# Float32r head sums for the removal keys, and mixer steps traced later among the big products, in a hybrid decoder layer

## The chip, the cores and the metric

The kernel runs on one core of one Trainium2 chip. The metric is the device time of one execution in microseconds, as the median of several runs. PE is the matmul engine, DVE the vector engine, ACT the scalar engine, POOL the GpSimd engine; SP is the engine whose queue starts the loads of the weights.

## The reference

One layer for 256 tokens of width 2048, in float32, with `p` the product of the normalised input with `w_in`:

```
x = x + 0.5 * swiglu(rms_norm(x, ffn1_norm), ...)           # inner width 5632
q, k, v, p_rwkv, gates = split(rms_norm(x, mix_norm) @ w_in)
y_attn = sliding_window_attention(q, k, v, sinks)           # 16 heads of 64, window 128
y_rwkv = rwkv7_time_mix(p_rwkv, ...)                        # 16 heads of 64
x = x + (gate_attn * (y_attn @ w_proj_attn) + gate_rwkv * (y_rwkv @ w_proj_rwkv)) @ w_out
x = x + cross_attention(rms_norm(x, cross_norm), mem)       # 256 rows of memory, 4 heads of 128
x = x + 0.5 * swiglu(rms_norm(x, ffn2_norm), ...)
return rms_norm(x, final_norm)
```

Within `rwkv7_time_mix` each of the 1024 columns of `k` is scaled, and then each head of 64 is divided by its length; this is where the sums of the removal keys come from:

```
kk = k * k_k
kk = kk / max(sqrt(sum(kk * kk over the head's 64 columns)), 1e-12)
```

The recurrence over the tokens has `-kk` and `kk * a` as the two vectors by which the state is corrected at each step (`a` and `b` in `S = S * w + (S a) b + v k`).

## The kernel before, in words

**Products.** Every large product is made of float32r matmuls. A value is split into `hi`, its float32r rounding, and `lo`, the rest, also float32r; `times` (L414 to L419) makes three matmuls of 512 columns out of it: `xh` with `hi` (L417), `xh` with `lo` (L418), `xl` with `hi` (L419). The weights come through SP's queue into `raw` tiles (`load`, L324 on), at most four ahead of use, and are split by an ACT copy (L344) and a DVE subtraction (L345), two items ahead of use. The feed-forward parts have their own variant with combined weights (L352, L353); the change does not touch it.

`product` (L393 on) goes through its weight items, each of two chunks of 128 rows. For each item it makes 6 matmuls for the tokens 0 to 127 and 6 for 128 to 255. Such six matmuls are called a **step** here. With `skew=True` the last three items are kept back, and then worked off for the first 128 tokens and afterwards for the others, without a tick.

**Ticks.** After each step `product` calls `bg.tick()`. `bg` holds generators in groups ("feat", "attn", "ew", "chain", "norm", "mem" and so on); a tick advances one to two of each group to its next `yield`. All mixer work that is not a big product is traced in this way, spread among the steps. `idle(n)` is `n` yields. So the yields set how many steps lie between two pieces of work, and the order of tracing gives each engine its in-order queue; a scheduler may move instructions a little against it. PE's queue above all is one line: a matmul that waits holds up the big matmuls behind it.

**The mixer's stages, in order,** run under the products with `w_in`, `w_proj_attn`, `w_proj_rwkv` and `w_out`:

- `shifted` (L910): transposes (in `feat`, L605) and token shift of the rwkv columns. The name "small" is the last 288 columns, needed by the decay.
- `removal_keys` (L1003 to L1072), for two heads' halves `h` in turn, on "ew": `kk`, its squares, the head sums with a constant of ones (`bdones`, L1022), root, maximum and reciprocal, the vectors `at` and `bt`, then in a loop over two blocks of 128 tokens the products of `kk` and `at` (L1059), masked on DVE (L1065) and stored by POOL's queue to `ld` in DRAM.
- `substitute` (L1075 to L1096), behind them on "ew": it loads 32x32 blocks from `ld` into `dl` (L1080, four DMAs of SP's queue), inverts them by forward substitution on DVE (a multiply L1087 and a reduction L1092 for each of 31 rows, a step or two apart) and stores them.
- The products of the attention's gate and of `ya`, the attention's output, with `w_proj_attn` (L1103 to L1113): for each of four column blocks a sigmoid and a DVE multiply (L1112).
- `values` (L1133) with two head sums per half by `head_sums` (L797 to L804, matmul L802) with `bdones_r`, the float32r copy of `bdones`.
- `pairs` (L1201 on), on "chain", two heads' columns at a time: masked products (L1190 the matmul, L1196 the mask on DVE), then the chain of small products which carries the state through both blocks.
- `finish` (L1322 on), on "norm": the group norm of `y` (L1341 root, L1343 reciprocal), the gate product L1349, L1353 to L1360, and the split into `yr` (L610, L611). `yr` is what the products with `w_proj_rwkv` read.
- The products with `w_out` into the `x2` blocks (L1414 to L1426): a DVE sum (L1421), then the next norm's transposes of this block, spawned on "feat".

`halves_of` (L793 to L796) splits a tile into float32r halves: a copy on ACT (L794) and a subtraction on DVE (L795). L1059 and L1190 use 64 rows of PE each, the upper or the lower; two that follow each other on different halves can run beside each other.

Of the kernel before, what the change touches and what calls it, by code (L numbers as in the profile page):

```python
# [8 lines left out]
F32R = mybir.dt.float32r  # L9
# [123 lines left out]
def decoder_layer(ctx: ExitStack, tc: tile.TileContext, a: dict, out: bass.AP):  # L133
# [34 lines left out]
    def idle(n):  # L168
        for _ in range(n):
            yield  # L170


    ones = cpool.tile([P, P], F32, name="ones")
# [17 lines left out]
    def mixer_constants(sp):  # L191
# [30 lines left out]
        for v in (bdones, bdmean):  # L222
            r = sp.tile([P, P], F32R, name="ones_r" + str(len(ones_r)))
            act.copy(r[:], v[:])
            ones_r.append(r)
        return abias, mask3, mask_l, bdones, ones_r, keep

# [544 lines left out]
    with tc.tile_pool(name="mx", bufs=1, reuse_waits="tile") as sp:  # L772
        aligned(sp)
        abias, mask3, mask_l, bdones, (bdones_r, bdmean), keep = mixer_constants(sp)

# [133 lines left out]

        def shifted(tok, cols, mus, outs, name):  # L910
            for q in range(0, len(cols), 2):
                n = len(cols[q : q + 2])
                b = feat(tok, cols[q : q + 2])
                p = sp.tile([P, 2, T + 1], F32, tag="p", name="p", bufs=2)
                pool.memset(p[:, :, 0:1], 0.0)
                act.copy(p[:, :n, 1:], b[:, :n])
                yield
                d = sp.tile([P, 2, T], F32, tag="d", name="d", bufs=2)
                pool.tensor_tensor(d[:, :n], p[:, :n, :T], p[:, :n, 1:], ALU.subtract)
                yield  # L920
                for i in range(n):
                    m = mu[:, mus[q + i] : mus[q + i] + 1]
                    dve.scalar_tensor_tensor(
                        outs[q + i], d[:, i, :], m, p[:, i, 1:], ALU.mult, ALU.add
                    )
            bg.seen.add(name)
# [81 lines left out]
        def removal_keys(h):  # L1008
# [8 lines left out]
            act.activation(sq[:], kk[:], AF.Square)  # L1017
            yield
            for i in (0, 2):
                b = tr()  # L1020
                sq2 = sq[:, i : i + 2, :].rearrange("p c t -> p (c t)")
                pe.matmul(b[:], bdones[:], sq2, start=True, stop=True)  # L1022
                act.activation(sq2, b[:], AF.Sqrt)
                yield
                dve.tensor_scalar(sq2, sq2, 1e-12, None, ALU.max)
                for k in range(2):
                    dve.reciprocal(sq[:, i + k, :], sq[:, i + k, :])
                    yield from idle(2)
# [23 lines left out]
            for c in range(2):  # L1052
# [17 lines left out]
                pool.dma_start(ld[:, o : o + 8, :], lt[:])  # L1070
                yield
            yield  # L1072


        def substitute():  # L1075
            yield from idle(4)
            dl = t4("dl", (P, 32, 32))
# [27 lines left out]
        for n in range(4):  # L1105
            pg = product(n2.x, W["w_in"])
            g = t4("ga", (P, 2, 512))
            for t in range(2):
                act.activation(g[:, t, :], pg[t][:], AF.Sigmoid, scale=n2.r[t])
            pa = product(ya, W["w_proj_attn"])  # L1110
            for t in range(2):
# [22 lines left out]
        def values(h):  # L1134
# [13 lines left out]
            for i in (0, 2):  # L1148
                b = head_sums(
                    bdones_r, [v[:, i : i + 2, :].rearrange("p c t -> p (c t)") for v in kp[h]]  # L1150
                )
                v2 = vv[:, i : i + 2, :]
                dve.tensor_tensor(v2, b[:].rearrange("p (c t) -> p c t", c=2), v2, ALU.mult)
                yield
# [48 lines left out]
        def pairs(h, q):  # L1203
# [11 lines left out]
            for c in range(2):  # L1215
                cs_ = slice(c * P, (c + 1) * P)
                if c == 0:
                    mk = masked(h, js, ((0, 0), (1, 0)))
                    yield
                    later = masked(h, js, ((2, 0), (2, 1)))  # L1220
                    yield
                vp = [vtok[h][:, c, j * P : (j + 1) * P] for j in js]
# [57 lines left out]
                if c == 0:  # L1280
                    mk_next = masked(h, js, ((0, 1), (1, 1)))
                    yield
                b = tr()
# [131 lines left out]
        for n in range(4):  # L1415
# [4 lines left out]
            for t in range(2):  # L1420
                dve.tensor_tensor(s[:, t, :], po[t][:], s[:, t, :], ALU.add)  # L1421
            bg.spawn("feat", n3.block(n, s))
            if n == 0:
# [156 lines left out]
```

## Time and profile before

| what | value |
| --- | --- |
| median of 3 runs | 2251.75 us (2251.66 to 2252.43) |
| the profiled execution | 2252.57 us |
| its span, from the first to the last instruction | 2250.8 us |
| mean granted PE clock | 0.999 |
| busy share: PE, DVE, ACT, POOL | 99%, 79%, 54%, 6% |
| chain that ended last: PE, DVE, DMA | 94%, 3%, 1% |

A row of the timeline has the start in microseconds, the duration, the engine, the line and operation, output and inputs with their shapes, the count of records and, in brackets, how long the engine was idle before it and what released it. The durations of matmuls are modelled and overlap; the distance between two starts is what counts. A matmul of plain float32 leaves two records. The stage table has the stretch, its length, and then for each engine the busy time and the count of records, in the order PE, PEld (weight load), DVE, ACT, POOL, then granted clock, DMA share and GB/s. The chain of waits is the work that ended last, followed back, with start and length.

### The profile page before, as it was taken

Reading aid. Unit: us, or ns where it says so; the run is one execution under the profiler, and the core shown is the slowest. Engines: PE = TensorE matmul, PEld = TensorE weight load, DVE = VectorE, ACT = ScalarE, POOL = GpSimd, SP = SyncE. Lnnn points to the kernel's source line nnn. Section 1 sums busy time; section 2 is a strip of 40 time slices with the busy share of each in tenths; the row PEclk is TensorE's granted clock in tenths of the full one; section 3 lists DMA queues with packets and bytes.
Section 4 is the critical chain, followed back from the end, with each engine's and each line's share of the span. In section 5 each row is a group of like instructions: output and inputs, shape, how many; then the busy total and the mean of one; then the engine's idle time right before and its main releaser. Section 6 shows DMA issues by size and latency. Waiting matters only on the chain.

```text
span 2250.8 us, 28046 instructions
## 1 busy us (share of the span) xinstructions
PE 2235.2 (99%) x10617; PEld 1840.3 (82%) x10617; DVE 1782.0 (79%) x2279; ACT 1226.5 (54%) x1601; POOL 132.6 (6%) x192
## 2 busy tenths in 40 slices
PE   9999999999999999999999999999999999999998
PEld 7888888888888877788888888888888888888886
DVE  7898988998989476887534566557998988998987
ACT  6555555555556467444444446556555555554554
POOL 1000000000001000301220040001000000000002
PEclk9999999999999999999999999999999999999999
DMA  7555555556556544676523476548565565555564
GB/s 263 187 201 201 197 203 202 193 190 216 192 188 205 163 142 150 201 223 212 166 77 109 163 261 227 186 159 284 185 213 187 195 210 194 190 209 200 189 207 147
DMA packets 219143, 432.49 MB, mean 192 GB/s; under 512 B 14107, under 2 KB 16384, under 8 KB 219008
## 3 DMA queue, kind: packets, MB, share of 16 engines
q1 hardware_dynamic: 210432, 404.78, 53.3%
q0 software_dynamic: 8112, 25.12, 3.5%
q8 instruction: 83, 1.36, 0.2%
q10 hardware_dynamic: 464, 0.79, 0.1%
q14 instruction: 52, 0.43, 0.1%
HBM read 417.56 MB, written 13.11 MB: 191 GB/s over the span
## 4 chain that ended last, share of the span: by engine, by line
PE 94%; DVE 3%; DMA 1%; issue 1%; POOL 1%; ACT 0%; SPq 0%; POOLq 0%; DVEq 0%; ACTq 0%
PE acc L417 19%; PE acc L418 19%; PE acc L419 19%; PE mm L419 8%; PE mm L418 8%; PE mm L417 8%; PE tr L605 2%; PE tr L418 2%; PE tr L419 2%; PE tr L417 2%; PE mm L1254 1%; DVE lo L345 1%; PE tr L1190 1%; DMA raw<-in_w_out_dram 0%; PE mm L844 0%
## 5 line engine op out<-in xcount | busy, mean ns | idle before, releaser
L345 DVE TENSOR_TENSOR lo<-raw,hi 128x1024 fp32r<-128x1024 f32 (+1 forms) x770 | 894.5, 1163 | 336.6 <-ACT hi L344 334.4
L344 ACT CAST hi<-raw 128x1024 fp32r<-128x1024 f32 (+1 forms) x770 | 759.3, 997 | 734.7 <-PE acc L419 519.6
L417 PE MATMUL acc<-hi,xhi 128*128 128x512 f32 (+1 forms) x1196 | 474.3, 397 | 2.4 <-ACT xhi L632 1.9
L418 PE MATMUL acc<-lo,xhi 128*128 128x512 f32 (+1 forms) x1196 | 464.8, 389 | 0.0
L419 PE MATMUL acc<-hi,xlo 128*128 128x512 f32 (+1 forms) x1196 | 464.1, 388 | 0.0
L417 PEld LDWEIGHTS acc<-hi,xhi 128*128 128x128 f32 x1196 | 225.0, 188 | 51.4 <-issue 4.0
L419 PEld LDWEIGHTS acc<-hi,xlo 128*128 128x128 f32 x1196 | 224.5, 188 | 46.9 <-DVE xlo L633 1.0
L418 PEld LDWEIGHTS acc<-lo,xhi 128*128 128x128 f32 x1196 | 224.9, 188 | 45.3 <-issue 1.7
L352 ACT CAST thi<-raw 128x1024 fp32r<-128x1024 f32 x172 | 178.9, 1050 | 60.4 <-DVE raw L373 46.5
L353 DVE TENSOR_TENSOR tlo<-raw,thi 128x1024 fp32r<-128x1024 f32 x172 | 208.3, 1220 | 0.7 <-ACT thi L352 0.4
L417 PE MATMUL mm<-hi,xhi 128*128 128x512 f32 x380 | 149.3, 393 | 0.0
L419 PE MATMUL mm<-hi,xlo 128*128 128x512 f32 x380 | 148.2, 390 | 0.0
L418 PE MATMUL mm<-lo,xhi 128*128 128x512 f32 x380 | 148.2, 390 | 0.0
L418 PE MATMUL acc<-lo,hhi 128*128 128x512 f32 x372 | 145.6, 391 | 0.8 <-DVE lo L345 0.8
L419 PE MATMUL acc<-hi,hlo 128*128 128x512 f32 x372 | 145.6, 391 | 0.0
L417 PE MATMUL acc<-hi,hhi 128*128 128x512 f32 x372 | 144.9, 390 | 0.0
L419 PEld LDWEIGHTS mm<-hi,xlo 128*128 128x128 f32 x380 | 71.3, 188 | 14.8
L418 PEld LDWEIGHTS mm<-lo,xhi 128*128 128x128 f32 x380 | 71.4, 188 | 14.5
L417 PEld LDWEIGHTS mm<-hi,xhi 128*128 128x128 f32 x380 | 71.4, 188 | 14.5
L418 PEld LDWEIGHTS acc<-lo,hhi 128*128 128x128 f32 x372 | 69.9, 188 | 15.5 <-DVE lo L345 1.2
L417 PEld LDWEIGHTS acc<-hi,hhi 128*128 128x128 f32 x372 | 69.9, 188 | 14.3
L419 PEld LDWEIGHTS acc<-hi,hlo 128*128 128x128 f32 x372 | 69.9, 188 | 14.0
(392 smaller groups left out, 3511.9 us busy)
## 6 DMA issues: line engine op xcount, KB each, us to landing
raw<-in_ffn_w_up_dram SPq DMA_DIRECT2D x88, 1024.0 KB, 5.4
raw<-in_ffn_w_down_dram SPq DMA_DIRECT2D x88, 1024.0 KB, 5.1
raw<-in_ffn_w_gate_dram SPq DMA_DIRECT2D x84, 1024.0 KB, 5.1
raw<-in_w_in_dram SPq DMA_DIRECT2D x136, 512.0 KB, 3.5
raw<-in_w_out_dram SPq DMA_DIRECT2D x32, 512.0 KB, 4.5
raw<-in_w_proj_attn_dram SPq DMA_DIRECT2D x16, 512.0 KB, 3.9
raw<-in_w_proj_rwkv_dram SPq DMA_DIRECT2D x16, 512.0 KB, 5.7
raw<-in_w_cross_kv_dram SPq DMA_DIRECT2D x16, 512.0 KB, 3.6
```

Source lines behind the costliest of these rows:

```text
L344: at["hi"] = act.copy(hi[:, s], raw[:, s])
L345: at["lo"] = dve.tensor_tensor(lo[:, s], raw[:, s], f32(hi[:, s]), ALU.subtract)
L352: act.copy(hi[:], v[:])
L353: dve.tensor_tensor(lo[:], v[:], f32(hi[:]), ALU.subtract)
L417: pe.matmul(o, xh, hi, start=first, stop=False, **how)
L418: pe.matmul(o, xh, lo, start=False, stop=False, **how)
L419: pe.matmul(o, xl, hi, start=False, stop=last, **how)
L605: pe.transpose(b[:, o : o + P], tok[:, t, col : col + P], ident[:])
L1190: pe.matmul(b[e][:, o : o + P], x1[r, j, cs_], x2[r, j, cs_], start=True, stop=True)
L1254: pe.matmul(vb[:, (o + k) * P : (o + k + 1) * P][:, r], lhs(k, e), rhs[:, k, r], start=first and k + e == 0, stop=True, **ek,)
```

## The change

1. `mixer_constants` no longer returns the plain float32 `bdones` next to its float32r copy; the copy takes the name `bdones`. `values` uses it as before.
2. `removal_keys` splits the squares into float32r halves (`sh`, `sl`, one ACT copy and one DVE subtraction of 128x1024 for each half `h`), waits two ticks in place of one, and makes each of the four sums by `head_sums`, two float32r matmuls, in place of one matmul of plain float32.
3. In the loop over the two blocks `removal_keys` waits two ticks in place of one behind each block.
4. `shifted` begins two ticks later for "small".
5. `substitute` waits ten ticks in place of four before its loads.
6. The fourth product of `ya` with `w_proj_attn` is skewed, so six of its eight steps have no tick.
7. `pairs` waits two ticks in place of one behind the masks `later` and `mk_next`.
8. The norm of each `x2` block is spawned with two ticks of waiting ahead (`later_by`).

In the order of the instructions the counts change by 4 matmuls on PE, 3 instructions on ACT and 2 on DVE.

```diff
+    def later_by(n, steps):
+        yield from idle(n)
+        yield from steps
...
-        return abias, mask3, mask_l, bdones, ones_r, keep
+        return abias, mask3, mask_l, ones_r, keep
...
-        abias, mask3, mask_l, bdones, (bdones_r, bdmean), keep = mixer_constants(sp)
+        abias, mask3, mask_l, (bdones, bdmean), keep = mixer_constants(sp)
...
         def shifted(tok, cols, mus, outs, name):
+            if name == "small":
+                yield from idle(2)
...
             act.activation(sq[:], kk[:], AF.Square)
-            yield
+            sp_ = halves_of(sq[:], t4("sh", dt=F32R)[:], t4("sl", dt=F32R)[:])
+            yield from idle(2)
             for i in (0, 2):
-                b = tr()
                 sq2 = sq[:, i : i + 2, :].rearrange("p c t -> p (c t)")
-                pe.matmul(b[:], bdones[:], sq2, start=True, stop=True)
+                b = head_sums(
+                    bdones, [v[:, i : i + 2, :].rearrange("p c t -> p (c t)") for v in sp_]
+                )
                 act.activation(sq2, b[:], AF.Sqrt)
...
                 pool.dma_start(ld[:, o : o + 8, :], lt[:])
-                yield
+                yield from idle(2)
             yield
...
         def substitute():
-            yield from idle(4)
+            yield from idle(10)
...
-            pa = product(ya, W["w_proj_attn"])
+            pa = product(ya, W["w_proj_attn"], skew=n == 3)
...
                     later = masked(h, js, ((2, 0), (2, 1)))
-                    yield
+                    yield from idle(2)
...
                     mk_next = masked(h, js, ((0, 1), (1, 1)))
-                    yield
+                    yield from idle(2)
...
-            bg.spawn("feat", n3.block(n, s))
+            bg.spawn("feat", later_by(2, n3.block(n, s)))
```

More of the change, by code (lines that the diff above doesn't have):

```diff
@@ L1149, in values @@
                 b = head_sums(
-                    bdones_r, [v[:, i : i + 2, :].rearrange("p c t -> p (c t)") for v in kp[h]]
+                    bdones, [v[:, i : i + 2, :].rearrange("p c t -> p (c t)") for v in kp[h]]
                 )
```

## The prediction

> **What bounds the kernel now.** I read the page first (its engines, clock and chain), then PE's timeline for the gaps between big matmuls, then DVE's and ACT's around each gap.
>
> ```profile
> span 2250.8 us, 28046 instructions
> PE 2235.2 (99%) x10617; PEld 1840.3 (82%) x10617; DVE 1782.0 (79%) x2279; ACT 1226.5 (54%) x1601; POOL 132.6 (6%) x192
> ...
> PEclk9999999999999999999999999999999999999999
> ...
> PE 94%; DVE 3%; DMA 1%; issue 1%; POOL 1%; ACT 0%; SPq 0%; POOLq 0%; DVEq 0%; ACTq 0%
> ...
> L345 DVE TENSOR_TENSOR lo<-raw,hi 128x1024 fp32r<-128x1024 f32 (+1 forms) x770 | 894.5, 1163 | 336.6 <-ACT hi L344 334.4
> L344 ACT CAST hi<-raw 128x1024 fp32r<-128x1024 f32 (+1 forms) x770 | 759.3, 997 | 734.7 <-PE acc L419 519.6
> ```
>
> PE is busy for 99% of the span and the chain that ended last is PE's for 94%. So time comes only from small PE work made cheaper, or from gaps of PE closed, and time goes wherever PE waits anew. The unit is the spacing of big matmuls:
>
> ```profile
> 1293.36 0.39 PE L417 MATMUL acc<-hi,yrhi 128*128 128x512 f32 x1
> ...
> 1301.52 0.39 PE L417 MATMUL acc<-hi,yrhi 128*128 128x512 f32 x1
> ```
>
> These are the first matmul of the product of `yr` and the one 36 later, which first reads the last two of its eight chunks: 8.16 us / 36 = 0.227 us each, and six of them, one step between two ticks, are 1.36 us. The change leaves all 8958 of these big matmuls as they are. A gap is below the distance of two starts less 0.23.
>
> **The change part by part.** The instruction order of the two kernels, compared engine by engine, gives the places.
>
> *Four sums (L1022).* The chain of waits shows one in the old form, and one of L802 in the form that takes its place, on the same tile shape:
>
> ```profile
> 887.85 0.86 PE tr L1022 x2
> ```
>
> ```profile
> 1143.42 0.46 PE tr L802 x2
> ```
>
> 0.40 each, **gain 1.6**. The price is two casts and two subtractions more for the two heads, 2 x (1.0 on ACT + 1.16 on DVE) by the means of L344 and L345, which have the same shape. The stage covers it:
>
> ```profile
> 880.00:955.00 75.00, 74.70 (x362) 59.35 (x361) 64.48 (x70) 40.96 (x48) 17.96 (x13) 1.00 0.61 193
> ```
>
> DVE has 64.5 of 75 us taken, so 2.3 more fit; without that cover a late `lo` would cost up to 2.3. I cost it at nothing.
>
> *Transposes of the small columns (two steps later).*
>
> ```profile
> 815.01 0.40 PE L419 MATMUL acc<-hi,xlo 128*128 128x512 f32 x1
> 816.16 0.33 PE L605 MATMUL tr<-ident,tok 128*128 128x128 f32 x1 [0.75 <-ACT tok L788]
> ...
> 821.21 0.40 PE L419 MATMUL acc<-hi,xlo 128*128 128x512 f32 x1
> ...
> 821.88 0.44 PE L605 MATMUL tr<-ident,tok 128*128 128x128 f32 x2 [0.27 <-DVE yalo L899]
> ```
>
> 1.15 - 0.23 = 0.92 and 0.67 - 0.23 = 0.44. They move by 1 and by 0.5 step (1.36 and 0.68 us), more than the gaps: **gain 1.36**.
>
> *Pair products of the removal keys (L1059), two steps apart instead of one.*
>
> ```profile
> 910.44 1.16 PE L1059 MATMUL mm<-kk,at 64*128 64x128 f32 x16
> ...
> 912.66 0.48 PE L1059 MATMUL mm<-kk,at 64*128 64x128 f32 x2
> 913.43 1.16 PE L1059 MATMUL mm<-kk,at 64*128 64x128 f32 x14 [0.29 <-DVE lt L1065]
> ```
>
> ```profile
> 947.83 1.65 PE L1059 MATMUL mm<-kk,at 64*128 64x128 f32 x16
> ```
>
> The first 16 take 1.16. The second 16 take 1.93 from 912.66 to 914.59, stopped by the masked copy that frees their bank, and the second head's 1.65: 0.77 + 0.49, **gain 1.26**. But in the new order one of the four groups is split by row half, and one pair of another is torn apart, so that there upper and lower 64 rows no longer run side by side. Before there are 16 side-by-side pairs and no single, after it 11 pairs and 10 singles.
>
> ```profile
> 1183.98 1.08 PE tr L1190 x8
> ...
> 1235.90 1.09 PE tr L1190 x16
> ```
>
> Here 8 records (4 matmuls, alone) cost what 16 (4 pairs) cost, 0.27 a matmul or a pair. So each broken pair costs 0.27: 5 x 0.27, **loss 1.35**. The masks of `pairs` (L1190) go the other way, 29 pairs to 33: 4 x 0.27, **gain 1.08**.
>
> *Masks (`idle(2)` for `yield` in `pairs`).*
>
> ```profile
> 1110.68 0.40 PE L419 MATMUL acc<-hi,xlo 128*128 128x512 f32 x1
> ...
> 1111.39 1.75 PE L1190 MATMUL tr<-rt,kk 64*128 64x128 f32 x16 [0.31 <-DVE mk L1196]
> ...
> 1113.07 0.51 PE L417 MATMUL acc<-hi,xhi 128*128 128x512 f32 x1
> ```
>
> 2.39 from matmul to matmul, against 0.23 + 1.09 without a wait, is 1.07. A step more is 1.36, but the DVE copy it waits for can be late behind a weight's `lo` (1.16) as well. Bounds 0 and 1.07; I take half, **gain 0.5**.
>
> *The fourth product of `ya`, skewed.*
>
> ```profile
> 1018.68 0.39 PE L419 MATMUL acc<-hi,xlo 128*128 128x512 f32 x1
> 1019.49 0.50 PE L417 MATMUL acc<-hi,xhi 128*128 128x512 f32 x1 [0.43 <-DVE ga L1112]
> ```
>
> ```profile
> 1007.33 0.81 DVE L1087 TENSOR_TENSOR tmp<-xt,dl 128x625 f32<-128x625 f32 x1
> 1008.17 0.81 DVE L1092 TENSOR_REDUCE xt<-tmp 128x25 f32<-128x625 f32 x1
> ...
> 1018.75 1.28 DVE L1112 TENSOR_TENSOR ga<-acc,ga 128x512 f32<-128x512 f32 x2
> ```
>
> The next product waits for the banks that L1112 reads: 0.81 - 0.23, **gain 0.58**, as the first half now ends 18 matmuls (4.08 us) ahead. The skewed passes have no ticks, so all mixer work behind them comes 6 steps later, beside the six of `substitute` and the three more of each `removal_keys`: 18 in all. And DVE has its 0.64 multiply, two L1087 and one L1092 of about 0.83 and then a `lo` of 1.16 in a row: 4.3 us from 0.17 after the first pass (a matmul's record less its spacing), with gaps 4.6, while PE wants that `lo` at 4.08 + 0.23 = 4.31. **Loss 0.3** (0 to 1.2, one `lo`).
>
> *Blocks loaded six later.* The four loads of `dl` pass six weight loads in SP's queue. PE waits for neither in this stretch and DVE's substitution starts later as a whole: nothing either way. Its cover is the chain behind it, which is the next term.
>
> *The end of the chain.* 18 steps and some later, the last `finish` comes to the product of `yr`. Before, its last product L1349 starts at 1265.76; its result is needed at 1301.52, 28 us of slack.
>
> ```profile
> 1265.76 1.89 PE L1349 MATMUL tr<-xs,g 128*128 128x256 f32 x8
> ```
>
> ```profile
> 1263.96 3.35 DVE L1343 RECIPROCAL sq<-sq 128x512 f32<-128x512 f32 x1 [0.23 <-ACT sq L1341]
> ...
> 1269.82 0.87 DVE L1360 SCALAR_TENSOR_TENSOR yq<-yq,rv,tr 128x256 f32<-128x256 f32 x2
> ...
> 1273.00 0.69 DVE L611 TENSOR_TENSOR yrlo<-yq,yrhi 128x512 fp32r<-128x512 f32 x1 [1.18 <-ACT yrhi L610]
> ```
>
> ```profile
> 1270.47 1.28 ACT L1382 ACT_TABLE_LOAD   x1 [0.34 <-PE acc L419]
> 1271.77 0.69 ACT L1382 ACTIVATE gr<-acc,rs 128x512 f32<-128x512 f32 x1
> 1272.36 0.61 ACT L610 CAST yrhi<-yq 128x512 fp32r<-128x512 f32 x1
> ```
>
> In the new order L1349 stands 22 steps later (29.9 us), at step 829 of a need at 832; the scheduler puts 7 matmuls of the next product ahead of that need. From L1349's start PE has 1.5 (itself) + 3 x 1.36 + 7 x 0.227 = 7.2 us of work. The chain took 4.93 from there to the end of L1360. It gets one `lo` more (1.16), and its square root now stands on ACT behind the gates' ACTIVATEs and a table load, from 0 to 3.8 us (2 x 1.28 + 2 x 0.6); I take 1.8. With the cast of 0.61 and 0.1 to release it: 4.93 + 1.16 + 1.8 + 0.7 = 8.6, so PE waits 1.4. Behind it on PE stands the whole rest of the product. **Loss 1.4**, bounds 0 and 1.4 + 2.0 + 0.8 (a later `yrlo`) = 4.2.
>
> The Trainium skill, page "ScalarE: Activation LUTs", section "What ACT_TABLE_LOAD costs", puts a drain of about 1380 ns beside each load of 1283 ns. The trace has the 1.28 us load, but the ACTIVATE at 1271.77 stands directly behind it, so the row speaks for no drain; with two drains the tail would, by an estimate from that page, be 2.8 us later and the sum -1.8.
>
> *`x2` blocks two steps later.*
>
> ```profile
> 1363.60 0.39 PE L419 MATMUL acc<-hi,mtlo 128*128 128x512 f32 x1
> ...
> 1365.60 0.48 PE L417 MATMUL acc<-hi,mthi 128*128 128x512 f32 x1
> ...
> 1366.85 0.39 PE L419 MATMUL acc<-hi,mtlo 128*128 128x512 f32 x1
> ...
> 1367.43 0.48 PE L417 MATMUL acc<-hi,mthi 128*128 128x512 f32 x1
> ```
>
> Four transposes take 2.00 at the first block, when they wait for the sum on DVE, and 0.58 where they don't: **gain 1.42**. Those of the memory's and the last blocks then share a step: **loss 0.2** (0 to 0.5).
>
> **Sum.** Gains 1.60 + 1.36 + 1.26 + 1.08 + 0.5 + 0.58 + 1.42 = 7.80; losses 1.35 + 0.3 + 1.4 + 0.2 = 3.25; net -4.55. The profiled execution took 2252.57 us, its span and 1.77 around it, so it becomes 2248.0. The median of the runs is 0.82 below it: 2247.2.
>
> **The rivals.**
> 1. *The tail is hidden.* If ACT's order lets the square root through at once, the tail and the skew's `lo` cost nothing, and the masks' wait goes wholly: -4.55 - 1.4 - 0.3 - 0.57 = -6.8, 2244.9; without the other small losses 2243.7. For it: 28 us of slack before, and an estimate that is short by only 1.4.
> 2. *The waits only move.* The closed gaps are 1.36 + 1.26 + 0.58 + 0.5 + 1.42 = 5.1. Each wait is for an engine that also makes `hi` and `lo`; if half of them come back at the next step or as a late `lo`, it is 2249.8, if all, 2252.3. Against it: each move is longer than its gap.
> 3. *The tail decides, and the kernel is slower.* The last `finish` is in one line with PE once it is late: each us of it is one of the span. If its square root stands behind the whole ACT block (3.8), its reciprocal behind one more `lo` and the cast behind one `hi` and one more `lo` (3.3), PE waits 1.4 + 2.0 + 1.16 + 3.3 = 7.9 and the kernel ends at 2253.7. It is slower from a wait of 6.0 on. For it: the chain has no slack left; against it: two of its bounds must fall together. The Trainium skill, "TensorE: Matmul & The Clock Gate", section "What's actually happening", lets an idle window of about 3.4 us halve PE's clock, which would lengthen such a wait; here the granted clock is 9 in all 40 slices and no gap above reaches 2 us, so no row shows it.
> 4. *The sums do not get faster* in the new form, though the row of L802 has the same shape: 2248.8.
>
> **How the numbers follow.** The forecast has 0.36 (2246 to 2248.5), the hidden tail 0.25, the waits that move 0.23, the slow tail 0.13, the sums 0.03. A measurement of this kernel tells about 0.2%, 4.5 us, from no change; that border is 2247.25, in the middle of the forecast. Faster by more: 0.25 and somewhat over half of 0.36, 0.46; slower by more than 4.5 (past 2256.25): a third of the slow tail and a little for what I have not seen, 0.08; the rest, 0.46, is the same. The range goes from the hidden tail without small losses, 2243.7, to the upper bounds of tail, `lo` and masks together, -4.55 + 2.8 + 0.9 + 0.5 + 0.3 = 0, 2251.7.
>
> **What would show it.** The sums at L802 with 0.46 each at four more places. No bracket at the small columns' transposes, at the first `x2` transposes and at the first matmul after `ya`'s fourth product. L1059 in groups with 0.27 for each matmul that stands alone. A gap of 1 to 2 us ahead of the first matmul on the last chunk of `yr`, released by `yrhi`; none speaks for rival 1, one over 6 for rival 3. New brackets at L417 or L418 released by `hi` or `lo` between steps 573 and 900 speak for rival 2. The forecast is wrong if the big matmuls' spacing changes anywhere, or if a `raw` transfer releases PE.

## The result and the profile after

The changed kernel takes 2257.67 us (median of 7 runs, 2255.8 to 2260.36), the kernel before 2251.75 us (7 runs, 2251.32 to 2252.88). The ratio is 1.0026, 95% interval 1.0016 to 1.0036: slower by 5.9 us, where 4.6 us less were forecast. The profiled execution took 2256.07 us, 3.50 more than that of before.

The page of the changed kernel: span, engines, the shares of the chain that ended last.

```profile
span 2254.4 us, 28045 instructions
...
PE 2235.0 (99%) x10617; PEld 1839.1 (82%) x10617; DVE 1788.1 (79%) x2281; ACT 1230.6 (55%) x1604; POOL 131.5 (6%) x192
...
PE 94%; DVE 3%; issue 1%; ACT 1%; DMA 1%; SPq 0%; POOLq 0%; POOL 0%; DVEq 0%; ACTq 0%
```

PE's busy time is 0.2 us less and the span 3.6 us more, so in this execution the loss is in waits of PE. (Lines of the changed kernel stand 4 to 8 further down: L421 to L423 are the three matmuls, L348 and L349 `hi` and `lo`, L806 the head sums, L1067 the pair products, L1095 and L1100 the substitution's rows.) The view of PE's waits from 890 to 1420 us lists them, with the total, the times and the longest (before, the same view has four groups, together 2.0 us):

```profile
PE acc L422 <- DVE lo L349: 2.5, 2, 2.1
PE mm L1067 <- DVE lt L1073: 1.4, 1, 1.4
PE acc L421 <- ACT hi L348: 0.8, 1, 0.8
PE acc L421 <- DVE x L1429: 0.8, 1, 0.8
PE tr L1198 <- DVE mk L1204: 0.7, 2, 0.4
PE acc L421 <- ACT yrhi L614: 0.6, 1, 0.6
PE acc L421 <- DVE ga L1120: 0.5, 1, 0.5
```

The 8958 big matmuls are the same in both, so the start of the n-th can be compared. This table gives changed minus before at quiet places, and from that what each stretch cost (a step is six big matmuls):

| stretch of steps | what lies in it | forecast, us | measured, us |
| --- | --- | --- | --- |
| 560 to 605 | small columns' transposes | -1.36 | -0.53 |
| 605 to 645 | four sums, first half's pair products | -1.60 and about 0 | -1.82 |
| 645 to 660 | a wait for `hi`, second half's pair products | about 0 | +3.30 |
| 660 to 690 | first rows of the substitution | 0 | +2.46 |
| 690 to 705 | skewed product: `lo`, then `ga` | +0.3 and -0.58 | +0.64 and -0.59 |
| 705 to 845 | masks, pairs, last `finish` | -1.58 and +1.4 | +0.58 |
| 845 to the end | `x2` | -1.22 | -0.59 |

In the stretch with the last `finish`, the steps 830 to 836 cost 1.3 around the wait for `yrhi` (0.6 in its bracket, the rest in the gaps beside it); that leaves -0.8 for masks and pairs.

**The first loss (step 654).** PE, then DVE, then POOL of the changed kernel around 953:

```profile
957.07 1.16 PE L1067 MATMUL mm<-kk,at 64*128 64x128 f32 x8 [1.39 <-DVE lt L1073]
```

```profile
952.70 0.68 DVE L1120 TENSOR_TENSOR ga<-acc,ga 128x512 f32<-128x512 f32 x1
953.30 3.11 DVE L349 TENSOR_TENSOR lo<-raw,hi 128x1024 fp32r<-128x1024 f32 x1
956.34 1.27 DVE L1073 TENSOR_TENSOR lt<-mm,mask_l 128x512 f32<-128x512 f32 x2
```

```profile
952.96 2.36 POOL L1057 TENSOR_TENSOR kt<-kt,aa 128x1024 f32<-128x1024 f32 x1 [30.92 <-DVE aa L1053]
...
956.06 2.57 POOL L1058 TENSOR_TENSOR aa<-kt,cs 128x1024 f32<-128x1024 f32 x1
```

PE waits for the masked copy that frees its bank. That copy stands on DVE behind a `lo` that takes 3.11 us in place of 1.2. It ends at 956.41, which is 1.09 after POOL's product ends (955.32), so it looks as if the `lo` only began its work then. Both have two inputs in SBUF. The Trainium skill, page "SBUF — State Buffer", section "Who interferes with whom", says that such a pair shares a read port, that the one that starts first has it for its whole instruction, and that the other blocks; the trace agrees to 0.1 us. Before, `lo` came directly behind the scaling of `aa` and began first, and POOL's product was the longer one; DVE, then POOL of the kernel before:

```profile
945.16 1.38 DVE L1045 TENSOR_SCALAR aa<-aa,rv,ok_a 128x256 f32<-128x256 f32 x4
946.46 1.22 DVE L345 TENSOR_TENSOR lo<-raw,hi 128x1024 fp32r<-128x1024 f32 x1
```

```profile
946.72 3.18 POOL L1049 TENSOR_TENSOR kt<-kt,aa 128x1024 f32<-128x1024 f32 x1 [26.31 <-PE mm L1059]
```

Now `ga`'s multiply stands between, and POOL begins first.

**What else lies in the 3.30 (step 647).** PE and ACT of the changed kernel around 940, then ACT of the kernel before:

```profile
942.82 0.50 PE L421 MATMUL acc<-hi,xhi 128*128 128x512 f32 x1 [0.82 <-ACT hi L348]
```

```profile
936.05 1.28 ACT L1031 ACT_TABLE_LOAD   x1
937.35 0.60 ACT L1031 ACTIVATE sq<-tr 128x512 f32<-128x512 f32 x1
937.96 1.28 ACT L1117 ACT_TABLE_LOAD   x1
939.26 0.69 ACT L1117 ACTIVATE ga<-acc,rs 128x512 f32<-128x512 f32 x1
939.84 2.93 ACT L348 CAST hi<-raw 128x1024 fp32r<-128x1024 f32 x3
```

```profile
938.07 1.26 ACT L1109 ACTIVATE ga<-acc,rs 128x512 f32<-128x512 f32 x2
```

PE waits 0.82 for the last of three `hi`, and the stretch loses 1.1 there with the gap behind it. Before, the two sigmoids of `ga` stand together on ACT. Now a root of the head sums stands between them, with a table load of 1.28 on either side, and the three `hi` wait behind all of it. So of the 3.30, 1.1 is this wait and 1.39 the wait of the first loss. The other 0.8 is in the second group of pair products: what were 16 records side by side are now 8 and 8 alone, 1.1 us more, and one more turn between big and small matmuls, less the 0.5 that PE waited within this group before.

**The second loss (step 677).** PE, DVE and ACT around 989:

```profile
988.64 0.61 PE L421 MATMUL acc<-hi,xhi 128*128 128x512 f32 x2
991.40 0.50 PE L422 MATMUL acc<-lo,xhi 128*128 128x512 f32 x1 [2.14 <-DVE lo L349]
```

```profile
984.76 0.69 DVE L1120 TENSOR_TENSOR ga<-acc,ga 128x512 f32<-128x512 f32 x1 [1.77 <-PE acc L423]
986.12 0.69 DVE L1120 TENSOR_TENSOR ga<-acc,ga 128x512 f32<-128x512 f32 x1 [0.67 <-PE acc L423]
986.73 0.15 DVE L1095 TENSOR_TENSOR tmp<-xt,dl 128x1 f32<-128x1 f32 x1
...
989.69 0.23 DVE L1095 TENSOR_TENSOR tmp<-xt,dl 128x64 f32<-128x64 f32 x1
990.12 1.22 DVE L349 TENSOR_TENSOR lo<-raw,hi 128x1024 fp32r<-128x1024 f32 x1 [0.20 <-ACT hi L348]
```

```profile
983.40 1.05 ACT L348 CAST hi<-raw 128x1024 fp32r<-128x1024 f32 x1 [1.67 <-PE acc L423]
```

The `hi` of this item was ready at 984.45. Its `lo` starts at 990.12 (the bracket names a later `hi`). In DVE's order there stand ahead of it the two multiplies of `ga`, which wait for the end of a product, and then 15 instructions of the first eight rows of the substitution, 3.2 us in one piece. In the kernel before only one of these instructions comes ahead of the next `lo`, then six:

```profile
971.13 0.15 DVE L1087 TENSOR_TENSOR tmp<-xt,dl 128x1 f32<-128x1 f32 x1
972.59 1.23 DVE L345 TENSOR_TENSOR lo<-raw,hi 128x1024 fp32r<-128x1024 f32 x1 [1.30 <-ACT hi L344]
```

### The profile page after: what moved, and what is told of

Its sections match the earlier page's. It is cut to its first block, busy times and chain, and to the rows that moved or that the text cites. A ratio compares the mean times of both kernels' runs of the same rounds, so it can differ in the third digit from the quotient of the medians.

```text
span 2254.4 us, 28045 instructions
## 1 busy us (share of the span) xinstructions
PE 2235.0 (99%) x10617; PEld 1839.1 (82%) x10617; DVE 1788.1 (79%) x2281; ACT 1230.6 (55%) x1604; POOL 131.5 (6%) x192
## 3 DMA queue, kind: packets, MB, share of 16 engines
q8 instruction: 83, 1.36, 0.2%
## 4 chain that ended last, share of the span: by engine, by line
PE 94%; DVE 3%; issue 1%; ACT 1%; DMA 1%; SPq 0%; POOLq 0%; POOL 0%; DVEq 0%; ACTq 0%
PE acc L421 19%; PE acc L423 19%; PE acc L422 19%; PE mm L422 8%; PE mm L423 8%; PE mm L421 8%; PE tr L609 2%; PE tr L422 2%; PE tr L421 2%; PE tr L423 2%; PE mm L1262 1%; DVE lo L349 1%; PE tr L1198 1%; PE mm L848 0%; DMA raw<-in_w_out_dram 0%
## 5 line engine op out<-in xcount | busy, mean ns | idle before, releaser
L349 DVE TENSOR_TENSOR lo<-raw,hi 128x1024 fp32r<-128x1024 f32 (+1 forms) x770 | 897.0, 1167 | 340.3 <-ACT hi L348 338.4
L348 ACT CAST hi<-raw 128x1024 fp32r<-128x1024 f32 (+1 forms) x770 | 759.3, 997 | 737.2 <-PE acc L423 534.7
L421 PE MATMUL acc<-hi,xhi 128*128 128x512 f32 (+1 forms) x1196 | 472.9, 396 | 2.9 <-ACT xhi L636 1.6
L423 PE MATMUL acc<-hi,xlo 128*128 128x512 f32 (+1 forms) x1196 | 464.4, 389 | 0.0
L421 PEld LDWEIGHTS acc<-hi,xhi 128*128 128x128 f32 x1196 | 224.9, 188 | 51.5 <-issue 3.0
L423 PEld LDWEIGHTS acc<-hi,xlo 128*128 128x128 f32 x1196 | 224.5, 188 | 47.1 <-DVE xlo L637 1.0
L421 PE MATMUL mm<-hi,xhi 128*128 128x512 f32 x380 | 149.3, 393 | 0.0
L423 PE MATMUL mm<-hi,xlo 128*128 128x512 f32 x380 | 148.2, 390 | 0.0
L423 PE MATMUL acc<-hi,hlo 128*128 128x512 f32 x372 | 145.5, 391 | 0.0
L421 PE MATMUL acc<-hi,hhi 128*128 128x512 f32 x372 | 144.9, 390 | 0.0
L423 PEld LDWEIGHTS mm<-hi,xlo 128*128 128x128 f32 x380 | 71.3, 188 | 14.9
L421 PEld LDWEIGHTS mm<-hi,xhi 128*128 128x128 f32 x380 | 71.4, 188 | 14.5
L421 PEld LDWEIGHTS acc<-hi,hhi 128*128 128x128 f32 x372 | 69.9, 188 | 14.3
L423 PEld LDWEIGHTS acc<-hi,hlo 128*128 128x128 f32 x372 | 69.9, 188 | 13.9
```

The lines of the kernel that those rows point to most:

```text
L348: at["hi"] = act.copy(hi[:, s], raw[:, s])
L349: at["lo"] = dve.tensor_tensor(lo[:, s], raw[:, s], f32(hi[:, s]), ALU.subtract)
L421: pe.matmul(o, xh, hi, start=first, stop=False, **how)
L423: pe.matmul(o, xl, hi, start=False, stop=last, **how)
```

## The experiments

Each edit is against the changed kernel, or against the run named. The runs are called e1 to e12 below: e1 and e2 move the loads and the substitution, e3 POOL's products, e4 takes one tick back, e5 has the sums alone, e6 the small columns and `x2`; e7, e8, e10, e11 and e12 start from e4 (substitution, skew, masks, `x2`, substitution), and e9 from e5. Every median is of 11 runs; the kernel before ran beside them, with medians of 2252.1, 2251.72 and 2251.91 in the three groups.

### The loads of dl six steps earlier, the rows traced where they were

```diff
         def substitute():
-            yield from idle(10)
+            yield from idle(4)
...
-            yield from idle(14)
+            yield from idle(20)
             tmp = t4("tmp", (P, 32, 32))
```

> The changed kernel with the loads of dl issued after 4 ticks as before the change, and 20 ticks in place of 14 behind them, so that the substitution itself is traced where the change puts it. In the order of DVE its first eight rows then follow six lo's and no longer stand behind the two multiplies of ga. Theory A (a lo stands in DVE's queue behind ga's multiply, which waits for the end of a product, and behind eight rows of the substitution): the 2.14 us wait of PE for lo at 988.9 goes, the span is 2.2 to 2.5 us shorter than the changed kernel's, some 2253.7 by its profiled run. Theory B (the loads of dl themselves collide with the weights on their way): they still pass the queue at a busy place, and a wait of 1 us or more for a raw or a lo stays near the loads. The last finish stays where the change has it, so its waits of about 1.5 us stay. If the lower granted clock of the other runs of the changed kernel (0.996 to 0.998, up to 4 us longer) comes from the long wait at 988.9, the runs lie within 1 us of each other here; if it comes from the waits of the last finish, they still spread over 3 to 4 us.

2254.03 us (2253.34 to 2256.61). The wait at step 677 is gone: the stretch 660 to 690 costs 0.0 in place of 2.46. Though the rows are traced at the old place, they are scheduled earlier with their loads: they run from 976.28, behind six `lo` and ahead of both multiplies of `ga`, in place of 986.73. In the changed kernel `dl` had landed by 979.67, 7 us ahead of its rows, so the loads did not hold them up there. So the order on DVE was the cause. The expectation on the spread fell: the runs still lie 3.3 us apart, so the long wait at 989 alone does not make it. The trace shows another place, in the stage table (granted clock: third figure from the end of the row):

```profile
958.00:958.50 0.50, 0.50 (x3) 0.41 (x2) 0.50 (x1) 0.00 (x0) 0.50 (x1) 0.56 0.90 156
...
961.00:961.50 0.50, 0.50 (x3) 0.40 (x2) 0.50 (x1) 0.00 (x0) 0.36 (x1) 0.53 0.77 164
```

Here the clock is near half of full from 958.1 to 961.5, behind the first wait, the 1.39 us at the pair products, and the stretch 645 to 660 costs 4.9 in place of 3.3.

### All of the substitution six steps earlier

```diff
-            yield from idle(10)
+            yield from idle(4)
```

> The changed kernel with substitute's idle(10) back at idle(4): loads, substitution and all behind them six steps earlier. Theory A: the wait at 988.9 goes (2.4 us) and the last finish is done six steps ahead of need, so its waits (1.5 us) go too: about 3.9 us less than the changed kernel, some 2252.2 by its profiled run, and no run with a lower clock. Rival (the end of the chain has hardly a part in it): the same as the run with the loads alone earlier, within 0.5 us.

2253.59 us (2252.19 to 2255.65), span 3.7 us below the changed kernel's; the 2.46 at the rows are gone, and the stretch 705 to 845 is at -0.25 in place of +0.58. In it the steps 830 to 836 cost 0.0 in place of 1.3, but masks and pairs gain 0.25 in place of 0.8. Between this run and the one before, only 0.8 us of that stretch tells, and 0.4 by the medians: the tail is a small matter. The spread of 3.5 us is there without any wait for `yrhi`, so the last `finish` alone is not what makes it, and the expectation that no run would have a lower clock fell.

### POOL's products behind the masked copies

```diff
-            for i in range(4):
-                c = 4 * h + i
-                dve.tensor_scalar(
-                    aa[h][:, i, :], aa[h][:, i, :], k_a[:, c : c + 1], ok_a[:, c : c + 1],
-                    ALU.mult, ALU.add,
-                )
-            pool.tensor_tensor(kt[h][:], kt[h][:], aa[h][:], ALU.mult)
-            pool.tensor_tensor(aa[h][:], kt[h][:], ei[:], ALU.mult)
             for c in range(2):
...
                 yield from idle(2)
+            for i in range(4):
+                c = 4 * h + i
+                dve.tensor_scalar(
+                    aa[h][:, i, :], aa[h][:, i, :], k_a[:, c : c + 1], ok_a[:, c : c + 1],
+                    ALU.mult, ALU.add,
+                )
+            pool.tensor_tensor(kt[h][:], kt[h][:], aa[h][:], ALU.mult)
+            pool.tensor_tensor(aa[h][:], kt[h][:], ei[:], ALU.mult)
             yield
```

> The changed kernel with the scaling of aa (L1053) and POOL's two products (L1057, L1058) traced behind the loop of the pair products, so that they start after the masked copies. Theory A (POOL's product, begun at 952.96, holds up the lo that DVE begins at 953.30 until it has ended, 3.11 us in place of 1.2, so the masked copy behind it and PE wait): that lo takes 1.2, the wait of 1.39 us at the pair products goes, 1.4 us less, 2256.3; a lo that meets POOL later takes 2 to 3 us, at a place where no PE waits. Rival (the order on DVE, with two multiplies of ga ahead, makes the masked copy late): the wait stays at 1 us or more. The wait at 988.9 and the spread of the runs stay as they are.

2253.81 us (2253.26 to 2256.1). DVE and POOL of this run:

```profile
952.15 1.21 DVE L349 TENSOR_TENSOR lo<-raw,hi 128x1024 fp32r<-128x1024 f32 x1
...
960.71 2.08 DVE L349 TENSOR_TENSOR lo<-raw,hi 128x1024 fp32r<-128x1024 f32 x1 [1.27 <-ACT hi L348]
```

```profile
958.38 3.32 POOL L1077 TENSOR_TENSOR kt<-kt,aa 128x1024 f32<-128x1024 f32 x1
```

The first `lo` takes 1.21 again, though both multiplies of `ga` still stand ahead of it, so the rival falls. The stretch 645 to 660 costs 1.1 in place of 3.3, and that is the wait for `hi` at step 647 alone. The later `lo` meets POOL and ends at 962.79, again 1.09 after POOL's product (961.70), and PE doesn't wait for it. So POOL's product beside the `lo` was the cause of the 1.39 us. (The edit also takes most of the scaling of `aa` from ahead of the masked copy; but the hold of 3.11 - 1.2 = 1.9 is by itself longer than the wait.) In this trace the long wait of step 677 is followed by a slow stretch of PE:

```profile
989.38 0.50 PE L422 MATMUL acc<-lo,xhi 128*128 128x512 f32 x1 [2.15 <-DVE lo L349]
...
990.20 0.57 PE L422 MATMUL acc<-lo,xhi 128*128 128x512 f32 x1
...
993.55 0.45 PE L422 MATMUL acc<-lo,xhi 128*128 128x512 f32 x1
```

```profile
990.00:990.50 0.50, 0.50 (x3) 0.42 (x2) 0.50 (x1) 0.00 (x0) 0.00 (x0) 0.75 0.37 49
...
993.50:994.00 0.50, 0.50 (x3) 0.41 (x2) 0.00 (x0) 0.50 (x1) 0.00 (x0) 0.83 0.87 324
```

From about 990.2 to 993.6 the clock is 0.50. The eight matmuls from 990.20 to 993.55 take 3.35 us in place of 8 x 0.227 = 1.82: 1.5 us lost. That is also why the profile of this run is only 0.8 us below the changed kernel's: its execution had this stretch, that one had none. By the medians it is 3.9 less, where 1.4 were expected. The trace has 2.2 of it in the stretch 645 to 660: the wait, and the second half's pairs, which stand side by side again in two groups of 16. The fastest runs of the two kernels are 2.5 apart (2255.8 and 2253.26). The rest would fit fewer stretches of low clock in the median run, but no trace shows that.

### One tick again behind the pair products

```diff
                 pool.dma_start(ld[:, o : o + 8, :], lt[:])
-                yield from idle(2)
+                yield
```

> The changed kernel with one tick in place of two behind each block of pair products in removal_keys. All behind it comes four steps earlier. The pair products are in groups of 16 as before the change; the multiplies of ga stand behind the first masked copy on DVE again and a lo comes directly after the scaling of aa. By the first forecast this gives back 1.26 us of waits and takes away 1.35 of lost pairs, so nothing. Theory A: the loss of 3.3 us at the second half's pair products (1.39 of wait, 1.35 of pairs, the rest in the group's new place) goes, and with the four steps the eight rows do not stand behind ga either, so the 2.4 us go as well, and a part of the waits of the last finish: 5 to 6 us less, some 2251 by the profiled run.

2249.91 us (2248.83 to 2250.86), ratio to before 0.999 (0.9981 to 0.9999), span 5.3 us below the changed kernel's. The stretch 645 to 660 costs 0.8 in place of 3.3 and 660 to 690 1.0 in place of 2.46. The wait for `hi` at step 647 is gone, as the root stands ahead of both sigmoids again, and the wait at the pair products is 0.2, as DVE's `lo` begins ahead of POOL's product again. The pairs did not come back as expected: the second half runs as 16, 8 and 8 records. This one edit, counted as nothing in the forecast, turns the change from a loss to a small gain. The runs lie 2.0 us apart.

The 1.0 left in the stretch 660 to 690 belongs to this execution: two later runs of the same code up to there (masks back, three ticks for `x2`) have 0.0. Here `dl`'s four loads are mixed in SP's queue with those of `w_proj_attn`; the second of these weights landed at 972.38, against 970.50 with the masks back, and the rows on DVE waited for `dl` until 975.59, with a `lo` behind them. So the loads of `dl` can cost PE up to 1 us, too, by when they land.

### The sums alone, and the sums with the later loads

The kernel before with the sums' part of the change:

```diff
...
             act.activation(sq[:], kk[:], AF.Square)
-            yield
+            sp_ = halves_of(sq[:], t4("sh", dt=F32R)[:], t4("sl", dt=F32R)[:])
+            yield from idle(2)
             for i in (0, 2):
-                b = tr()
                 sq2 = sq[:, i : i + 2, :].rearrange("p c t -> p (c t)")
-                pe.matmul(b[:], bdones[:], sq2, start=True, stop=True)
+                b = head_sums(
+                    bdones, [v[:, i : i + 2, :].rearrange("p c t -> p (c t)") for v in sp_]
+                )
...
```

> The kernel before with the float32r head sums alone (the halves of the squares, two ticks behind them, head_sums in place of the plain float32 matmul); no other step is moved. The first forecast: four sums at 0.40 less each, 1.6 us less than the kernel before, with the two casts and two subtractions hidden. Rival (the shift of one tick for each half brings POOL's products into the way of a lo, as in the changed kernel): the 1.6 us are eaten by a wait of 1 to 2 us at the pair products, and the time is that of before or above.

2256.44 us (2254.98 to 2256.69), 4.7 above before: the rival's side, but at another place than it named. ACT of this run, and PE:

```profile
972.37 0.69 ACT L1111 ACTIVATE ga<-acc,rs 128x512 f32<-128x512 f32 x1 [5.75 <-PE acc L419]
973.73 0.69 ACT L1111 ACTIVATE ga<-acc,rs 128x512 f32<-128x512 f32 x1 [0.67 <-PE acc L419]
974.31 2.93 ACT L344 CAST hi<-raw 128x1024 fp32r<-128x1024 f32 x3
```

```profile
975.40 0.73 PE L417 MATMUL acc<-hi,yahi 128*128 128x512 f32 x2 [1.71 <-ACT hi L344]
976.66 0.80 PE L418 MATMUL acc<-lo,yahi 128*128 128x512 f32 x1 [0.53 <-DVE lo L345]
977.26 0.63 PE L419 MATMUL acc<-hi,yalo 128*128 128x512 f32 x1
```

ACT stands 5.75 us at a gate (the sigmoid of `ga`) that waits for the end of a product, with three `hi` behind it that the next product needs. PE waits 1.7 + 0.5, and its clock falls again (0.63 long records). The eight rows are in one piece on DVE here, too, but they end at 973.4, and the next `lo` then waits 1.96 for its `hi`, so the rows are not what holds PE. The weights of the next product play a part: in SP's queue all four loads of `dl` stand ahead of all four of `w_proj_attn`, whose first landed at 972.67. Its `hi` starts at 974.31, so the gates make 1.6 of the 1.7. The four sums themselves came as forecast, 0.45 each.

The same with the substitution later as in the change:

```diff
-            yield from idle(4)
+            yield from idle(10)
             dl = t4("dl", (P, 32, 32))
```

> The kernel before with the float32r head sums and substitute's idle(10), no other step moved. With the sums alone two gates (ga) stand on ACT ahead of three hi's that the next product waits for, and eight rows of the substitution on DVE ahead of the lo; here the eight rows follow seven lo's and the gates stand two hi's later. Theory A (the place of these rows against the end of a product is what costs): the 4.4 us lost at 975 to 979 in the run with the sums alone are gone, and the four sums' 1.6 to 1.8 are left: 2250.1, about 6 us less than with the sums alone. Rival (the casts and subtractions of the sums themselves are what delays DVE and ACT there): 2255 or above remains.

2250.55 us (2249.76 to 2252.43), 1.4 below before and 5.9 below the sums alone. So what the sums save is about what was forecast, and the casts are not what cost. The edit moves more than the rows: on ACT two more `hi` stand ahead of the gates, and in SP's queue two loads of `w_proj_attn` pass ahead of three of `dl`, so the first `hi` starts at 969.25. This run doesn't part these two orders; by the times of the run before, the gates count most.

### The small columns and x2 alone

Against the kernel before:

```diff
...
         def shifted(tok, cols, mus, outs, name):
+            if name == "small":
+                yield from idle(2)
...
-            bg.spawn("feat", n3.block(n, s))
+            bg.spawn("feat", later_by(2, n3.block(n, s)))
```

> The kernel before with the two ticks ahead of the small columns' shift and ahead of the norms of the x2 blocks, and nothing else. The first forecast: 1.36 + 1.42 - 0.2, so 2.6 us less. By the trace of the changed kernel only 0.4 + 0.6 of it comes, 1.0 us less: at the small columns two groups of the attention that stood together are parted, and at x2 the wait for the sum on DVE comes back at the first matmul of the next product (0.81).

2251.02 us (2250.59 to 2251.97), 0.7 below before, ratio 0.9998 (0.9989 to 1.0006): not told apart from nothing by the interval; the span is 0.7 less as well. The two reasons can be read in PE's timeline, of the kernel before and of the changed one:

```profile
818.14 1.52 PE L891 MATMUL tr<-pt,vt 128*64 128x256 f32 x12
```

```profile
815.39 1.08 PE L895 MATMUL tr<-pt,vt 128*64 128x256 f32 x6
...
817.99 1.08 PE L895 MATMUL tr<-pt,vt 128*64 128x256 f32 x6
...
1368.90 0.50 PE L421 MATMUL acc<-hi,mthi 128*128 128x512 f32 x1 [0.81 <-DVE x L1429]
```

Twelve records of the attention's product ran in 1.52 us as one group and are now two groups of 1.08. And the wait for the `x2` sum on DVE has moved from the transposes to the first matmul of the next product.

### Three further edits on top of one tick

Each starts from the run with one tick (2249.91).

```diff
         def substitute():
-            yield from idle(10)
+            yield from idle(4)
```

> The run with one tick between the blocks of pair products, and substitute's idle(10) back at idle(4) as well. If the queue of DVE at the pair products and at the first rows of the substitution was all that the later steps cost, and the last finish is four steps ahead of need already, six more steps bring nothing: the time of the run with one tick, 2249.9, within 0.5. If the later loads are still in the way, up to 1 us less. If substitution rows now meet the multiplies of ga at another product, 1 to 2 us more, with a bracket for lo.

2254.9 us (2253.23 to 2256.16), 5.0 more, a miss of the first expectation. Its trace repeats that of the sums alone: two gates on ACT ahead of three `hi`, a wait of 1.7 at 974.9, then matmuls 0.43 apart. Again all four loads of `dl` stand ahead of those of `w_proj_attn`. So `idle(10)` is worth 5 us with the sums and one tick, though in the changed kernel going back to `idle(4)` gained 4.

```diff
-            pa = product(ya, W["w_proj_attn"], skew=n == 3)
+            pa = product(ya, W["w_proj_attn"], skew=False)
```

> The run with one tick between the blocks of pair products, and the fourth product of ya not skewed. The skew gives 0.59 us at the multiplies of ga (its wait is gone in the trace of the changed kernel) and costs a wait for a lo (0.34 to 0.63 at 1016). Theory A: about 0.0 to 0.3 us difference to the run with one tick. Rival (the skew pays by the earlier ga): 0.6 us more, 2250.5.

2250.43 us (2249.43 to 2251.28), 0.5 more than with the skew, at the rival's side of the two; the spans are the other way round (2248.7 against 2249.1), so no more than that is told. The trace tells more of the reason: the wait of 0.59 for `ga` is gone without the skew as well, and the late `lo` of the skew with it (the stretch 690 to 705 is at -0.7, against 0.0 with the skew). The stretch up to step 830 then loses about as much (+0.2 against -0.8).

```diff
                     later = masked(h, js, ((2, 0), (2, 1)))
-                    yield from idle(2)
+                    yield
...
                     mk_next = masked(h, js, ((0, 1), (1, 1)))
-                    yield from idle(2)
+                    yield
```

> The run with one tick between the blocks of pair products, and one tick in place of two behind later and mk_next in pairs, as before the change. By the forecast the two ticks give 0.5 of wait and 1.1 of side-by-side pairs: 1.6 us more than the run with one tick, 2251.5. By the ledger of the changed kernel's trace about 1.0: 2250.9. If the pairs and waits come out alike either way: 2249.9.

2250.07 us (2249.33 to 2250.38): alike. The two ticks behind the masks bring nothing; the forecast had 1.6. In the trace the stretch 705 to 830 is at -0.6 without them and -0.8 with them, so most of this gain isn't theirs.

### Towards a better version

Both again start from the run with one tick.

```diff
-            bg.spawn("feat", later_by(2, n3.block(n, s)))
+            bg.spawn("feat", later_by(3, n3.block(n, s)))
```

> The run with one tick between the blocks of pair products, and three ticks in place of two ahead of the norms of the x2 blocks. Theory A (the wait of 0.5 to 0.8 us at the first matmul behind an x2 sum is for the banks that the sum on DVE reads, whatever the transposes do): nothing changes there, 2249.9 within 0.4. Rival (the transposes still wait): 0.5 us less, 2249.4. It is also the attempt at a version below both kernels.

2249.95 us (2248.78 to 2251.1): nothing gained at the median, though the wait at the first matmul is not in its view of waits any more. It is missing, too, in the runs with the loads of `dl` earlier and without the skew, whose `x2` steps are those of the changed kernel, so the third tick isn't shown to have done it.

```diff
         def substitute():
-            yield from idle(10)
+            yield from idle(7)
```

> The run with one tick between the blocks of pair products and substitute's idle at 7, between the 4 that cost 5 us and the 10 that did not. In the order of DVE the eight rows follow six lo's, no multiply of ga beside them; on ACT the gates stand one hi later than with 4. Theory A: without a product's end in front of the rows the time is that of the run with one tick, 2249.9, within 0.7, and no wait for hi or lo above 0.7 us. Rival (a late landing of dl costs by itself, the earlier the loads the more): half of the loss, 2252.5.

2248.94 us (2247.83 to 2250.1), ratio to before 0.9986 (0.9978 to 0.9995). It has the lowest median of all, below both kernels, though its range overlaps with that of the run with one tick. PE's longest waits from 570 to 1420 us:

```profile
PE mm L1067 <- DVE lt L1073: 0.6, 2, 0.4
PE acc L422 <- DVE lo L349: 0.5, 1, 0.5
PE acc L421 <- DVE x L1429: 0.4, 1, 0.4
```

With `idle` at 4, 7 and 10 the times are 2254.9, 2248.9 and 2249.9. That is no trend with the loads' time. At 4 the two gates stand on ACT ahead of three `hi`, and all loads of `dl` ahead of those of `w_proj_attn`; at 7 one `hi` and one load of `w_proj_attn` go ahead, at 10 two of each, and PE doesn't wait for a `hi` there. So what counts is the place in a queue, ACT's or SP's; the two were not tested apart.

## Why the prediction was wrong

**The first step that failed** is "Blocks loaded six later: nothing either way". The prediction asked whether PE waits for these loads; what counted was the queue of DVE, where the first eight rows are in one piece and now stand behind a product's end with a `lo` behind them. It cost 2.46 us, and moving the loads, and with them the rows, took all of it away (e1).

**The second, and the larger, is the pair products**, counted at -1.26 + 1.35. The first half gave nothing, as its wait came back as one for `ga` (0.5). The stretch of the second half cost 3.3: the 1.39 us wait, which is POOL's hold (e3), 1.1 at a wait for `hi` behind a root that came between two sigmoids, and 0.8 for lost pairs and parted groups. Both waits are gone with one tick (e4). The forecast named the masked copy as what frees the bank, but not that the copy's place on DVE, behind `ga` and a blocked `lo`, would change; and it priced ACT's part of the sums at its busy time, not at its order among the gates.

**The third is the clock.** Rival 3 held that no row shows it, as before it was 9 in all slices. It falls to 0.50 for about 3.4 us in some executions after a wait of 1.1 to 2.2 us, at 1.5 us each. The changed kernel's profiled execution has no such stretch ahead of its last 20 us, but its seven runs go from 2255.8 and 2256.07 (mean granted clock 0.999) over 2257.36, 2257.67 and 2258.15 (0.998) and 2258.94 (0.997) to 2260.36 (0.996). So the 1.6 of the median above the profiled run fit one such stretch, and the 4.6 between the fastest run and the slowest would be three of them, more than there are waits over 1 us; at which waits they fell isn't seen, as only one of these runs was traced.

**What held:** the sums (1.6 forecast, 1.8 in the trace, 1.4 at the median of e9), the late `lo` in the skew (0.3 forecast, 0.64), and the tail of the last `finish` (1.4 forecast, 1.3, though only 0.6 of it in the bracket of `yrhi`). The wait at `ga` (0.58 and 0.59) came out by luck: without the skew it is gone as well (e8). Rival 2 was the nearest: of the waits removed, those at `x2` and the small columns came back by half at the next step, and by its own sign there are new brackets released by `hi` or `lo` at the steps 647, 677 and 695. But it ended at 2252.3, with the old waits back; the new ones are longer than those removed. The masks' 1.6 were 0.8 in the trace and nothing in e10. With -4.55 forecast and +3.50 measured in the profiled executions, 8.05 are to explain: 2.46 (rows), 3.2 (stretch of the second half's pairs), 0.8 (small), 0.6 (`x2`), 0.8 (masks), 0.3 (`lo` in the skew), less 0.2 (sums) and 0.1 (tail), together 7.9. One figure of the prediction doesn't come out of its terms: without the other small losses (1.35 and 0.2) rival 1 ends at 2243.4, not 2243.7; nothing hangs on it.

## What to carry to other kernels

When steps are moved, don't ask only whether the moved engine work fits, but what stands behind each moved instruction in its in-order queue: an instruction that waits for the end of a product, put ahead of a `hi` or `lo`, can cost PE most of the wait (1.7 and 2.1 us here). A wait of PE can be worth more than its length: behind waits from 1.1 us on the clock fell in some executions. And a delay that helps in one place is worth nothing by itself: in the changed kernel 4 ticks were better than 10, and with one tick behind the pair products worse by 5 us; so such numbers are tried together, not one by one.

## What the runs showed of the hardware

A wait of 1.14 us (e9, at 1122.9), 1.39 us (e1) or 2.15 us (e3) was followed by a granted clock of 0.50 over some 3.4 us; in the changed kernel's traced execution neither 1.39 nor 2.14 was. The Trainium skill, "TensorE: Matmul & The Clock Gate", section "What's actually happening", gives the same length for the window and the same halving, but asks for an idle window of about 3.4 us; here shorter waits were enough in some executions. A DVE subtraction of 128x1024 with both inputs in SBUF that began 0.34 us after a POOL product took 3.11 us in place of 1.2, ending 1.09 after POOL's; before the change, where DVE began first, POOL's product was the longer one (3.18 in place of 2.36).
